# First modulation set in quarters, zero products on TensorE, split row statistics behind the experts, and a new table of priorities

## The chip, the cores and the metric

The kernel runs on one core of one Trainium2 chip. The metric is the device time of one execution in microseconds, the median of some runs. The engines of the core are TensorE (PE in the profile, its weight loads PEld), VectorE (DVE), ScalarE (ACT), GpSimd (POOL) and SyncE (SP), which issues nearly all of the loads.

## The reference

The input is 256 rows of 1024 (`x`), two conditioning vectors and 256 context rows for each of two blocks. Everything is float32. In short:

```python
# block 1
mod = silu(c) @ w_mod + b_mod            # 6 x 1024: sh1 sc1 g1 sh2 sc2 g2
h   = rmsnorm(x, norm1_g) * (1 + sc1) + sh1     # and hc from ctx, with c_ctx
y   = gated_linear_attention(h, hc)      # h @ w_in gives q, k, v, r; gates from w_gate_a, w_gate_b
x   = x + g1 * y
h2  = rmsnorm(x, norm2_g) * (1 + sc2) + sh2
f   = moe(h2)                            # 16 experts, top 2 of the best group of 4
x   = rmsnorm(x + g2 * f, final_g)
# block 2, two layers, each with its own modulation and a context branch
x, xc = ab_layer(x, ctx_2)               # latent attention and grouped attention, gated
x, xc = cd_layer(x, xc)                  # window attention and short convolution, gated
```

## The kernel before, in words

The weights lie in one flat array, cut on the host into pieces of 128 partitions and at most 2048 columns (1 MB), each loaded with one transfer from SyncE's queue. A dense product splits each float32 weight into a rounded part and a rest (`conv`: one ScalarE pass and one VectorE pass over 128x1024), and multiplies three combinations of parts in one-pass format, accumulating in PSUM. `Tjob` gives the product transposed (12 matmuls of 256 columns for each of 8 slices of the contraction), `tokjob` by rows (3 of 512 columns for each 128 rows and slice). The modulation vectors (`gemv`, `gemv_half`) keep float32, with 32 columns of stationary operand, four of them side by side in TensorE's columns.

Nothing runs in the order in which it is written. Every instruction is recorded with a place in the program (`Sched.rec`); stretches are interleaved (`merge`, `Blocks.order`), so that the context branch of block 2 (`cth`) is spread over the experts of block 1, and its last `TAIL` microseconds of TensorE work (`cth2`) are placed behind the experts, into section `t2`. Then `emit` walks through time with a cost for each instruction: an engine takes, among the instructions that could start first, the one with the lowest place plus `later`. `later` comes from the table `PRI`, one number for each section (`op.grp`) and one for each 24 instructions of it. The order found is the order in which each engine's queue, SyncE's included, gets its instructions; on the chip each engine works through its queue in order and waits on semaphores.

The start: `x` is loaded, its rows are normalised (`norm_rows`) and turned by 16 TensorE transposes. The first modulation set (shift and scale of block 1, 8 MB of `w_mod`) is computed in two halves, `gemv_half(0)` and `gemv_half(1)`, each of four 1 MB pieces; half h serves slices 4h to 4h+3 of the contraction. Behind each half one half of the q weights (`gq_h`) is loaded. A slice is modulated on its way out of the transposes' PSUM (`split_evac` under `trans`), multiplied into the gates' first factor (`lps`) and then used by the q, r, k and v products.

The end of the experts: `merge_y` adds each round's output to `facc` (= `x1`), by row tile and half. `overflow` is an instruction of all engines (a branch on a register that is read from memory) that may write `facc`. Then comes section `t2`: `facc` times the final gain (`xn2`), sums of squares of both, a chain of small VectorE instructions for the two reciprocal roots (`rsq`), and the modulated transposes for block 2 (`adaln_T`).

All compute instructions and most loads carry line 384 in the profile, since one helper issues them; the expert loads with an address from a register carry line 2066, and `overflow` line 2222. Rows are told apart by tile names: `w` weight pieces, `cs` the conditioning vectors, `cv` a split weight, `hlh`/`hll` and `hch`/`hcl` the modulated rows in two parts, `xn` is `xn2`.

## Time and profile before

| what | value |
|---|---|
| median of 3 runs | 892.22 us (892.08 to 894.15) |
| the profiled execution | 890.18 us, its span 888.4 us |
| TensorE busy | 844.4 us, 95% of the span |
| VectorE, ScalarE busy | 578.3 us, 416.4 us |
| weight loads of TensorE | 598.1 us (beside matmuls) |
| moved by DMA | 224.14 MB, mean 252 GB/s |
| mean granted TensorE clock | 0.991 |

Busy time of TensorE holds modelled ends of matmuls, so a stretch that is 100% busy may still hold short waits. Of 44 us in which TensorE is idle, most lies in three places: the first 27 us, the experts, and the very end. A wait with "DVEq L2222" or "PEq L2222" is one for the branch of `overflow`.

### The profile page before, as it was taken

Reading aid. Unit: us, or ns where it says so; the run is one execution under the profiler, and the core shown is the slowest. Engines: PE = TensorE matmul, PEld = TensorE weight load, DVE = VectorE, ACT = ScalarE, POOL = GpSimd, SP = SyncE. Lnnn points to the kernel's source line nnn. Section 1 sums busy time; section 2 is a strip of 40 time slices with the busy share of each in tenths; the row PEclk is TensorE's granted clock in tenths of the full one; section 3 lists DMA queues with packets and bytes.
Section 4 is the critical chain, followed back from the end, with each engine's and each line's share of the span. In section 5 each row is a group of like instructions: output and inputs, shape, how many; then the busy total and the mean of one; then the engine's idle time right before and its main releaser. Section 6 shows DMA issues by size and latency. Waiting matters only on the chain. (4 is left out here: it accounts for less than half of the span.)

```text
span 888.4 us, 15257 instructions
## 1 busy us (share of the span) xinstructions
PE 844.4 (95%) x5830; PEld 598.1 (67%) x5830; DVE 578.3 (65%) x1608; ACT 416.4 (47%) x819; POOL 0.9 (0%) x5
## 2 busy tenths in 40 slices
PE   4999999999999999999988995999999999999997
PEld 2677667767875656555633432688876778899986
DVE  2676889428984623444755424989866558899783
ACT  3466545226433222224444433555489715454890
POOL 0000000000000000000000000000000000000000
PEclk9999999999999999999999999899999999999999
DMA  9954961877526999999999998884713203465101
GB/s 381 415 217 181 377 252 58 303 327 285 189 100 229 416 357 374 342 386 371 360 416 373 403 420 317 315 355 143 281 52 142 96 1 142 167 248 204 49 1 48
DMA packets 32834, 224.14 MB, mean 252 GB/s; under 512 B 3568, under 2 KB 3824, under 8 KB 7408
## 3 DMA queue, kind: packets, MB, share of 16 engines
q1 hardware_dynamic: 32608, 222.56, 64.6%
q8 instruction: 48, 0.79, 0.3%
q0 software_dynamic: 144, 0.52, 0.2%
q14 instruction: 34, 0.28, 0.1%
HBM read 222.02 MB, written 1.05 MB: 251 GB/s over the span
## 5 line engine op out<-in xcount | busy, mean ns | idle before, releaser
L384 DVE TENSOR_TENSOR cv<-w,cv 128x1024 fp32r<-128x1024 f32 (+3 forms) x128 | 145.2, 1150 | 26.5 <-ACT cv L384 26.3
L384 ACT ACTIVATE cv<-w 128x1024 fp32r<-128x1024 f32 (+3 forms) x128 | 124.3, 998 | 57.6 <-DMA w<-in_w_dram 36.5
L384 PE MATMUL ps<-hh,cv 128*128 128x256 f32 x576 | 114.4, 288 | 0.2 <-ACT cv L384 0.2
L384 PEld LDWEIGHTS ps<-hh,cv 128*128 128x128 f32 x576 | 92.2, 191 | 5.9 <-issue 4.1
L384 PE MATMUL ps<-w,xg 128*32 128x512 f32 (+1 forms) x544 | 87.8, 605 | 3.3 <-DMA w<-in_w_dram 3.2
L384 PE MATMUL ps<-hl,cv 128*128 128x256 f32 x288 | 81.4, 285 | 0.0
L384 PE MATMUL ps<-cv,hh 128*128 128x512 f32 (+2 forms) x288 | 78.5, 352 | 0.4 <-ACT hh L384 0.4
L384 ACT ACTIVATE t<-ps 128x512 f32<-128x512 f32 (+5 forms) x77 | 36.0, 477 | 84.1 <-PE ps L384 67.4
L384 PE MATMUL ps<-c_col,t 128*128 128x128 f32 x384 | 63.0, 280 | 5.6 <-ACT t L384 4.9
L384 PEld LDWEIGHTS ps<-c_col,t 128*128 128x128 f32 x384 | 44.1, 141 | 33.8 <-ACT t L384 22.0
L384 ACT ACTIVATE t<-ps,s,f 128x512 f32<-128x512 f32 (+1 forms) x80 | 54.9, 690 | 18.6 <-DVE s L384 18.3
L384 PE MATMUL ps<-w,cs 128*32 128x512 f32 (+1 forms) x448 | 50.9, 563 | 12.8 <-DVE s L384 9.1
L384 PE MATMUL ps<-cv,mixh 128*128 128x512 f32 x192 | 60.7, 394 | 0.0
L384 DVE TENSOR_REDUCE s<-ps 128x1 f32<-128x512 f32 (+1 forms) x80 | 45.1, 580 | 20.3 <-PE ps L384 20.1
L384 PE MATMUL ps<-w,t 128*32 128x512 f32 (+1 forms) x320 | 54.2, 599 | 3.6 <-issue 3.0
L384 PEld LDWEIGHTS ps<-hl,cv 128*128 128x128 f32 x288 | 54.9, 191 | 2.8 <-issue 2.4
L384 PEld LDWEIGHTS ps<-cv,hh 128*128 128x128 f32 x288 | 49.7, 189 | 10.0 <-issue 2.4
L384 PEld LDWEIGHTS ps<-w,xg 128*32 128x32 f32 (+1 forms) x544 | 23.0, 118 | 47.1 <-issue 37.0
L384 PE MATMUL ps<-cv,hl 128*128 128x512 f32 (+2 forms) x144 | 49.0, 348 | 0.0
L384 ACT ACTIVATE PT<-ps 128x512 f32<-128x512 f32 (+1 forms) x80 | 39.3, 510 | 20.6 <-PE ps L384 20.3
L384 PE MATMUL ps<-cv,hlh 128*128 128x512 f32 x128 | 42.1, 403 | 0.0
L384 PEld LDWEIGHTS ps<-cv,mixh 128*128 128x128 f32 x192 | 35.7, 188 | 7.3 <-issue 0.4
(269 smaller groups left out, 1515.5 us busy)
## 6 DMA issues: line engine op xcount, KB each, us to landing
w<-in_w_dram SPq DMA_DIRECT2D x198, 1024.0 KB, 7.5
ctx<-in_ctx_dram SPq DMA_DIRECT2D x3, 1024.0 KB, 7.8
w<-in_w_dram SPq DMA_DIRECT2D x4, 576.0 KB, 8.3
x<-in_x_dram SPq DMA_DIRECT2D x2, 1024.0 KB, 7.2
w<-in_w_dram SPq DMA_DIRECT2D x4, 512.0 KB, 3.7
w<-in_w_dram SPq DMA_DIRECT2D x2, 768.0 KB, 9.5
out_dram<-x SPq DMA_DIRECT2D x2, 512.0 KB, 2.6
c_cst<-in_cst_dram SPq DMA_DIRECT2D x1, 528.0 KB, 14.8
```

The source lines that it names most:

```text
L384: op.fn = lambda: getattr(real, fn)(*a, **k)
```

## The change

The first modulation set is cut into four quarters of two 1 MB pieces (`modq{q}_{k4}`: four slices of the contraction with 128 columns for each of the four column groups). Quarter q serves slices 2q and 2q+1. Behind each quarter come, in program order, half-size loads (512 KB) of the q weights and of the first half of the r weights, one step of transposes (`trans_step`), and those slices' share of the two products. The bank pairs of both products (`pl`, `pr`) are held from the start. The scale is formed for both rows of modulation with one instruction a quarter (`A1`).

`busy` multiplies a tile of zeros into a PSUM bank that nothing reads (`idle`): 20 products of 512 columns ahead of the first quarter, and two of 256 columns after each of its eight slices.

Behind the experts the products with the final gain and the sums of squares are taken by halves of 512 columns, with one more addition. `TAIL` goes from 1 to 6. The r block is no longer interleaved with the context's modulation (`GLASEQ`).

The planner walks four times, each time over the order that the last walk found and with a table of its own (`PRIS`, four tables in place of one); nearly every number of the first table differs from `PRI`. It plans loads at 410 bytes a nanosecond instead of 380, and an expert load of 1 MB at 2557 ns instead of 2759 ns. The tables are cut here to their first lines.

```diff
--- before.py
+++ after.py
@@ -102,10 +102,10 @@
                 if b or s:
                     out[f"mod{b}_{s}_{kt}"] = m[:, kt, s * 2048:(s + 1) * 2048]
 
-    m = _kt(mods[0])[:, :, :2048].reshape(128, 8, 2, 2, 512)
-    for h in range(2):
-        for k2 in range(4):
-            out[f"modh{h}_{k2}"] = m[:, 2 * k2:2 * k2 + 2, :, h]
+    m = _kt(mods[0])[:, :, :2048].reshape(128, 8, 2, 4, 256)
+    for q in range(4):
+        for k4 in range(2):
+            out[f"modq{q}_{k4}"] = m[:, 4 * k4:4 * k4 + 4, :, q]
 
     def two(name, w):
         w = _kt(w)
...
-PRI = {
-    '': -1355, ('', 0): -400, ('', 2): 35, ('DB', 0): -400, ('DB', 3): -1630, ('DBc', 0): 1610, ('DG', 0): -210,
-    ('DG', 1): -100, ('DG', 2): 75, ('DG', 3): -265, ('DG', 4): -575, ('DGc', 0): 1575, ('Da', 1): -800,
...
-}
...
-TAIL = 1.0
+PRIS = [
+    {
+      '': -1160, ('DB', 0): -600, ('DB', 3): 370, ('DB', 4): 705, ('DG', 0): -160, ('DG', 1): 700, ('DG', 2): 110,
+      ('DG', 3): -365, ('DG', 4): -2170, ('DGc', 0): -800, ('Da', 1): -800, ('Da', 11): 3300, ('Da', 12): 1160,
...
+    },
+    {
+      '': 490, ('', 0): -590, ('', 1): -980, ('DB', 0): -45, ('DB', 1): -75, ('DB', 2): -2390, ('DB', 3): 1255,
+      ('DB', 4): -715, ('DBc', 0): -1390, ('DG', 0): 1715, ('DG', 1): -735, ('DG', 2): -1455, ('DG', 3): -400,
...
+    },
...
+TAIL = 6.0
...
@@ -277,6 +449,7 @@
 
 DMAW = 0.5
 XM = 0
+WARM = 20
 WPE = 0.0
 WACT = 40.0
 WDVE = 40.0
@@ -295,11 +468,11 @@
 NA = 8
 CTXSEQ = "CKgGqsk ba"
 CDSEQ = "kqc+x gB a+G o"
-GLASEQ = "N q r+M k+l1 K v+L+2 R+3 f"
+GLASEQ = "N q r M k+l1 K v+L+2 R+3 f"
 
 
 class Op:
-    __slots__ = ("eng", "fn", "acc", "cost", "lat", "preds", "npred", "succs", "tiles", "name", "later", "cols", "table", "grp", "tiled")
+    __slots__ = ("eng", "fn", "acc", "cost", "lat", "preds", "npred", "succs", "tiles", "name", "later", "cols", "table", "grp", "tiled", "key")
 
 
 class Sched:
@@ -409,7 +582,7 @@
     def _cost(self, eng, fn, out, a, k):
         n = self._free(out)
         if fn == "dma_start":
-            return out.partition_size() * n * 4 / 380.0
+            return out.partition_size() * n * 4 / 410.0
         if eng == "PE":
             r32 = a[1].dtype == F32R
             if fn == "transpose":
@@ -501,12 +674,21 @@
         out += lst[j:]
         self.cur[i0:i1] = out
 
-    def emit(self, reorder=True, window=3000):
-        ops = self.main
+    def emit(self):
+
         seen = {}
-        for op in ops:
+        for op in self.main:
             k = seen[op.grp] = seen.get(op.grp, -1) + 1
-            op.later += PRI.get(op.grp, 0) + PRI.get((op.grp, k // 24), 0)
+            op.key = op.grp, k // 24
+        for pri in PRIS:
+            for op in self.main:
+                op.later = pri.get(op.grp, 0) + pri.get(op.key, 0)
+            order = self._pass(self.main)
+            self.main = [self.main[i] for i in order]
+        for op in self.main:
+            op.fn()
+
+    def _pass(self, ops, window=3000):
         hist = {}
         for i, op in enumerate(ops):
             op.preds, op.succs = {}, []
@@ -527,10 +709,6 @@
                         h[:] = [x for x in h if x[0] == i or not (
                             r[0] <= x[1][0] and x[1][1] <= r[1] and r[2] <= x[1][2] and x[1][3] <= r[3])]
                 (hw if wr else hr).append((i, r))
-        if not reorder:
-            for op in ops:
-                op.fn()
-            return
         n = len(ops)
         for i, op in enumerate(ops):
             op.npred = len(op.preds)
@@ -698,10 +876,7 @@
                     ready[o2.eng].append(j)
         self.predicted = max(fin)
         self.busy = {e: sum(o.cost for o in ops if o.eng == e) for e in engs}
-        self.order, self.st = order, st
-        self.ret = {}
-        for i in order:
-            self.ret[i] = ops[i].fn()
+        return order
 
 
 class Blocks:
@@ -893,27 +1068,44 @@
             V.tensor_tensor(o[:, :, :, v], src[:, :, :, v], bias, op=OP.add)
         yield
 
-    def gemv_half(h):
+    A1 = fix([8, 2], F32, "f")
+    zero = t2([512], F32R, "z")
+    V.tensor_scalar(zero, cs[0].rearrange("p a b -> p (a b)")[:, 0:1].to_broadcast([128, 512]), 0.0, None, op0=OP.mult)
+    idle = psum()
+
+    def busy(n, w):
+
+        for _ in range(n):
+            mm(idle[:, :w], zero[:, :128], zero[:, :w], True, True)
+
+    sch.sec = "wu"
+    busy(WARM, 512)
+    sch.sec = ""
+
+    def gemv_quarter(q):
 
         ps = psum()
-        for k2 in range(4):
-            w = load(f"modh{h}_{k2}")
-            for kt in (2 * k2, 2 * k2 + 1):
+        for k4 in range(2):
+            w = load(f"modq{q}_{k4}")
+            for k in range(4):
+                kt = 4 * k4 + k
                 with sch.together():
                     for g in range(4):
-                        o = (kt % 2) * 1024 + g * 256
-                        mm(ps[32 * g:32 * g + 32, :256], cs[0][:, kt, :], w[:, o:o + 256], kt == 0, kt == 7)
-        r = t2([256])
-        S.activation(r, ps[:, :256], AF.Copy)
+                        o = k * 512 + g * 128
+                        mm(ps[32 * g:32 * g + 32, :128], cs[0][:, kt, :], w[:, o:o + 128], kt == 0, kt == 7)
+                    if q == 0:
+                        busy(2, 256)
+        r = t2([128])
+        S.activation(r, ps[:, :128], AF.Copy)
         pt = psum()
-        for j in range(2):
-            PE.transpose(pt[:, j * 128:(j + 1) * 128], r[:, j * 128:(j + 1) * 128], ident)
-        o = modc[:, 0, 0].rearrange("p (a h g j) v -> p a h g j v", a=2, h=2, g=2)[:, :, h]
-        bias = col("bm0")[:, :16].rearrange("p (a h g j) -> p a h g j", a=2, h=2, g=2)[:, :, h]
-        src = pt[:, :256].rearrange("p (j a g r) -> p a g j r", j=2, a=2, g=2)
-        for v in range(2):
-            for a in (1, 0):
-                V.tensor_tensor(o[:, a, :, :, v], src[:, a, :, :, v], bias[:, a], op=OP.add)
+        PE.transpose(pt[:, :128], r, ident)
+        o = modc[:, 0, 0].rearrange("p (a q j) v -> p a q j v", a=2, q=4)[:, :, q]
+        bias = col("bm0")[:, :16].rearrange("p (a q j) -> p a q j", a=2, q=4)[:, :, q]
+        V.tensor_tensor(o, pt[:, :128].rearrange("p (a j r) -> p a j r", a=2, j=2)[:, :, :, 0:2],
+                        bias[:, :, :, None].to_broadcast([128, 2, 2, 2]), op=OP.add)
+        c = slice(2 * q, 2 * q + 2)
+        V.scalar_tensor_tensor(A1[:, c, :], modc[:, 0, 0, 8 + 2 * q:10 + 2 * q, :], 1.0,
+                               col("n1")[:, c, None].to_broadcast([128, 2, 2]), op0=OP.add, op1=OP.mult)
 
     def modv(b, vec, v):
         s, h = divmod(vec, 2)
@@ -1003,14 +1195,17 @@
     def trans(tiles, fn):
 
         for k2 in range(4):
-            ps = psum()
-            for j in range(2):
-                for i in range(2):
-                    kt = 2 * k2 + j
-                    PE.transpose(ps[:, j * 256 + i * 128:j * 256 + i * 128 + 128],
-                                 tiles[i][:, kt * 128:(kt + 1) * 128], ident)
-            for j in range(2):
-                fn(2 * k2 + j, ps[:, j * 256:(j + 1) * 256])
+            trans_step(tiles, fn, k2)
+
+    def trans_step(tiles, fn, k2):
+        ps = psum()
+        for j in range(2):
+            for i in range(2):
+                kt = 2 * k2 + j
+                PE.transpose(ps[:, j * 256 + i * 128:j * 256 + i * 128 + 128],
+                             tiles[i][:, kt * 128:(kt + 1) * 128], ident)
+        for j in range(2):
+            fn(2 * k2 + j, ps[:, j * 256:(j + 1) * 256])
 
 
     def conv(src, tag="c"):
@@ -1508,31 +1703,46 @@
 
 
     norm_rows(xl, xl)
-    AB_ = [(fix([8], F32, "f"), modv(0, 0, v)) for v in range(2)]
-    wq = []
-    for h in range(2):
-        gemv_half(h)
-        for v in range(2):
-            c = slice(4 * h, 4 * h + 4)
-            V.scalar_tensor_tensor(AB_[v][0][:, c], modv(0, 1, v)[:, c], 1.0, col("n1")[:, c], op0=OP.add, op1=OP.mult)
-        wq.append(load(f"gq_{h}"))
-    (Al, Bl), (Ac, Bc) = AB_
+    sch.sec = "GM"
     xc = rows2("ctx", SY)
     hl, hc = new_hl("hl"), new_hl("hc")
     wga = col("wga").rearrange("p (k n) -> p k n", k=8)
-    lps = pd()
     bk = Blocks(sch, "G")
-    for (name, h, x_, A, B, o) in (("N", hl, xl, Al, Bl, 0), ("M", hc, xc, Ac, Bc, 256)):
-        bk(name)
-        if h is hc:
-            norm_rows(xc, xc)
-
+    bk("N")
+    lps, pl, pr = pd(), [pd(), pd()], [pd(), pd()]
+
+    def modulated(h, v, o):
         def fn(kt, ps):
             f = t2([256])
-            split_evac(ps, h.hi(kt), h.lo(kt), A[:, kt:kt + 1], B[:, kt:kt + 1], f, ALT and kt % 2)
+            split_evac(ps, h.hi(kt), h.lo(kt), A1[:, kt, v:v + 1], modv(0, 0, v)[:, kt:kt + 1], f, ALT and kt % 2)
             g = kt % 4
             mm(lps[32 * g:32 * g + 32, o:o + 256], wga[:, kt, :], f, kt < 4, kt >= 4)
-        trans(x_, fn)
+        return fn
+
+    early = {"gq": [Tjob(hl, pl)], "gr0": [tokjob(hl, t, pr[t]) for t in range(2)]}
+    blocks = {}
+    for q in range(4):
+        sch.sec = "G0"
+        gemv_quarter(q)
+        c2 = q % 2
+        for n in early:
+            off, ln = W["w"][f"{n}_{q // 2}"]
+            if not c2:
+                blocks[n] = b8([ln], n="w")
+            o_ = c2 * ln // 2
+            SY.dma_start(blocks[n][:, o_:o_ + ln // 2], bass.AP(
+                tensor=D["w"].tensor, offset=D["w"].offset + off + o_, ap=[[ln, 128], [1, ln // 2]]))
+        sch.sec = "GN"
+        trans_step(xl, modulated(hl, 0, 0), q)
+        for n, jobs in early.items():
+            sch.sec = "Gq" if n == "gq" else "Gr"
+            hi, lo = conv(blocks[n].rearrange("p (k n) -> p k n", n=512)[:, 2 * c2:2 * c2 + 2])
+            for k in range(2):
+                for j in jobs:
+                    j(2 * q + k, hi[:, k], lo[:, k], q + k == 0, 2 * q + k == 7)
+    bk("M")
+    norm_rows(xc, xc)
+    trans(xc, modulated(hc, 1, 256))
     low = t2([512], F32R), t2([512], F32R)
     split_evac(lps, *low)
 
@@ -1560,16 +1770,15 @@
     bk("q")
     kq = b8([2, 4, 256], n="kq")
     kT, qT = kq[:, 0], kq[:, 1]
-    pl = [pd(), pd()]
-    dense("gq", 512, [Tjob(hl, pl)], pre=wq)
     for i in range(2):
         S.activation(qT[:, 2 * i:2 * i + 2, :].rearrange("p b t -> p (b t)"), pl[i], AF.Copy, scale=128.0 ** -0.5)
 
     sr = b8([2, 1024], n="sr")
 
     def rproj(rh):
-        pss = [pd(), pd()]
-        dense(f"gr{rh}", 512, [tokjob(hl, 0, pss[0]), tokjob(hl, 1, pss[1])])
+        pss = [pd(), pd()] if rh else pr
+        if rh:
+            dense("gr1", 512, [tokjob(hl, 0, pss[0]), tokjob(hl, 1, pss[1])])
         for t in range(2):
             th = t2([512])
             S.activation(th, pss[t], AF.Tanh, scale=0.5)
@@ -2064,7 +2273,7 @@
             if r not in reg:
                 reg[r] = nc.values_load(eid[0:1, r:r + 1], engines=[mybir.EngineType.SP], min_val=0, max_val=NE - 1)
             nc.sync.dma_start(t, D["w"][bass.ds(reg[r] * step + off, 128 * ln)].rearrange("(p n) -> p n", p=128))
-        sch.special(f, [eid], [t], 2759.0, "SP")
+        sch.special(f, [eid], [t], 2557.0, "SP")
         return t
 
     def loads(ranks, *names):
@@ -2273,11 +2482,15 @@
 
     x2 = b8([2, 1024], n="x2")
     xn2 = b8([2, 1024], n="xn2")
+    s4 = sm([2, 2, 2])
+    for t in range(2):
+        for half in range(2):
+            c = slice(half * 512, half * 512 + 512)
+            V.tensor_tensor(xn2[:, t, c], facc[:, t, c], fg[:, c], op=OP.mult)
+            sumsq(facc[:, t, c], 512, s4[:, half, 0, t:t + 1])
+            (sumsqv if t else sumsq)(xn2[:, t, c], 512, s4[:, half, 1, t:t + 1])
     ss = sm([2, 2])
-    for t in range(2):
-        V.tensor_tensor(xn2[:, t], facc[:, t], fg, op=OP.mult)
-        sumsq(facc[:, t], 1024, ss[:, 0, t:t + 1])
-        (sumsqv if t else sumsq)(xn2[:, t], 1024, ss[:, 1, t:t + 1])
+    V.tensor_tensor(ss, s4[:, 0], s4[:, 1], op=OP.add)
     V.tensor_scalar(ss[:, 0], ss[:, 0], 1.0 / 1024, EPS, op0=OP.mult, op1=OP.add)
     V.tensor_scalar(ss[:, 1], ss[:, 1], 1.0 / 1024, None, op0=OP.mult)
     V.scalar_tensor_tensor(ss[:, 1], ss[:, 0], EPS, ss[:, 1], op0=OP.mult, op1=OP.add)
```

## Rows read from the trace of the kernel before

**Rows 1.** The page, engines' busy time, share of the span, instructions.

```profile
PE 844.4 (95%) x5830; PEld 598.1 (67%) x5830; DVE 578.3 (65%) x1608; ACT 416.4 (47%) x819; POOL 0.9 (0%) x5
```

**Rows 2.** Windows: stretch, length, busy time by engine (instructions), granted clock, DMA share, GB/s.

```profile
0.00:9.00 9.00, 0.00 (x0) 0.00 (x0) 3.60 (x17) 2.66 (x4) 0.20 (x4) 1.00 0.82 319
9.00:26.60 17.60, 14.36 (x130) 7.85 (x130) 6.38 (x21) 6.30 (x9) 0.00 (x0) 1.00 1.01 423
26.60:58.20 31.60, 31.60 (x209) 23.14 (x206) 21.06 (x51) 19.30 (x32) 0.00 (x0) 1.00 0.96 385
58.20:279.00 220.80, 219.01 (x1651) 160.46 (x1649) 160.51 (x394) 99.91 (x168) 0.65 (x1) 1.00 0.59 223
279.00:440.00 161.00, 159.98 (x1025) 92.98 (x1023) 74.31 (x177) 47.13 (x84) 0.00 (x0) 1.00 0.93 360
440.00:547.20 107.20, 91.68 (x620) 39.93 (x612) 49.95 (x186) 49.22 (x137) 0.00 (x0) 0.98 0.98 399
547.20:564.10 16.90, 10.83 (x50) 4.73 (x49) 11.70 (x29) 5.06 (x11) 0.00 (x0) 0.70 0.73 264
564.10:884.70 320.60, 316.90 (x2164) 269.02 (x2164) 250.75 (x739) 186.81 (x375) 0.00 (x0) 1.00 0.40 145
```

**Rows 3.** Waits of SyncE's queue, 279 to 548 us: in total, times, longest.

```profile
SPq L2066 <- PE ps L384: 167.9, 62, 10.7
```

**Rows 4.** Timeline of the first 45 us: start, duration, instructions, idle before.

```profile
9.08 1.93 PE L384 MATMUL ps<-w,cs 128*32 128x256 f32 x16 [9.08 <-DVE s L384]
...
12.30 3.46 PE L384 MATMUL ps<-c_col,x 128*128 128x128 f32 x15 [0.57 <-ACT x L384]
...
15.69 2.80 PE L384 MATMUL ps<-w,cs 128*32 128x256 f32 x48
...
22.72 0.50 PE L384 MATMUL ps<-hlh,cv 128*128 128x256 f32 x2
...
23.67 0.59 PEld L384 LDWEIGHTS ps<-w,cs 128*32 128x32 f32 x16
```

**Rows 5.** Timeline of TensorE, 45 to 62 us.

```profile
45.92 0.28 PE L384 MATMUL ps<-hll,cv 128*128 128x256 f32 x1
46.04 0.40 PE L384 MATMUL ps<-hlh,cv 128*128 128x256 f32 x2
...
46.28 0.63 PE L384 MATMUL ps<-cv,hlh 128*128 128x512 f32 x2
...
49.30 1.14 PE L384 MATMUL ps<-c_col,ctx 128*128 128x128 f32 x9
...
58.20 0.62 PE L384 MATMUL ps<-cv,hch 128*128 128x512 f32 x2
...
59.94 1.09 PE L384 MATMUL ps<-wgh,t 128*128 128x512 f32 x4
```

**Rows 6.** Timeline behind the last expert, 538 to 566 us.

```profile
547.82 2.49 DVE L384 TENSOR_TENSOR x<-x,ps 128x512 f32<-128x512 f32 x4
...
554.59 1.06 ACT L384 ACTIVATE junk<-x 128x1024 bf16<-128x1024 f32 x1 [7.96 <-DVEq L2222]
554.96 2.36 DVE L384 TENSOR_TENSOR xn<-x,fg 128x1024 f32<-128x1024 f32 x2 [4.65 <-DVEq L2222]
...
556.69 1.04 ACT L384 ACTIVATE junk<-xn 128x1024 bf16<-128x1024 f32 x1
...
557.36 1.22 DVE L384 SCALAR_TENSOR_TENSOR junk<-xn 128x1024 bf16<-128x1024 f32 x1
...
558.70 0.17 DVE L384 TENSOR_SCALAR s<-s 128x2 f32<-128x2 f32 x1
...
564.09 0.79 PE L384 MATMUL ps<-cv,hh 128*128 128x288 f32 x4 [0.36 <-ACT hh L384]
```

**Rows 7.** Timeline, 718 to 732 us: sums of squares over 512 columns.

```profile
719.61 0.64 ACT L384 ACTIVATE junk<-x 128x512 bf16<-128x512 f32 x1 [6.29 <-DVE x L384]
...
720.15 0.19 ACT L384 ACTIVATION_READ_ACCUMULATOR junk<-x 128x1 f32 x1
...
720.69 0.68 DVE L384 SCALAR_TENSOR_TENSOR junk<-x 128x512 bf16<-128x512 f32 x1
```

More of the change, by code (lines that the diff above doesn't have):

```diff
@@ L205 @@
 LEAD = 0
-PRI = {
[52 rows of a table removed]
-    'Xbw': 1225, 'Xg': 200, 'Xgc': -970, 'Xk': -105, 'Xkc': -600, 'Xq': 650, 'Xqc': -895, 'Xs': 3675, 'Xsc': 425,
[3 rows of a table removed]
-}
-TAIL = 1.0
+PRIS = [
+    {
[47 rows of a table added]
+      'Dcc': -160, 'Dg': -785, 'Dgc': 10, 'Dkc': -2490, 'Do': 10875, 'Doc': 165, 'Dq': -1220, 'Dqc': 10,
[9 rows of a table added]
+    },
+    {
[38 rows of a table added]
+      ('goc', 0): 300, ('hot', 0): -1405, ('hot', 1): 855, ('moe0', 0): -610, ('moe0', 1): -4775,
[11 rows of a table added]
+      'Lsc': 1590, 'XC': -5, 'XCc': 2130, 'XGc': -1240, 'XK': -50, 'XKc': 800, 'Xa': 245, 'Xb': -210, 'Xbw': 710,
[4 rows of a table added]
+    },
+    {
[56 rows of a table added]
+    },
+    {
[52 rows of a table added]
+    },
+]
+TAIL = 6.0
 APART = 1
```

266 rows, old and new, of tables (PRI, PRIS) are left out of this document.

## The prediction, made before the changed kernel ran

> **What bounds the kernel now.** I read the page's busy times first: TensorE is busy for 844.4 of 888.4 us [rows 1], so only 44 us can come from filling its idle time, unless busy time itself shrinks. The windows by stage come next [rows 2]. TensorE waits 9.0 us for the first weight piece, another 3.2 (17.60 less 14.36) until 26.6 us, and then hardly at all until 440: 1.8 us from 58 to 279, 1.0 from 279 to 440. In the experts' second part (440 to 547) it is idle for 15.5 us while DMA runs at a share of 0.98, and in the 16.9 us behind the last expert for 6.1. From 564 on it is idle for 3.7. So the start is bound by loads, the middle and the last 320 us by TensorE's order, the experts by both: over 279 to 547 the DMA share is 0.93 and then 0.98, 254.8 us of transfers in 268.2 us. The 13.4 us that are missing are SyncE's: it waits 167.9 us in that stretch for TensorE to free a weight buffer [rows 3], and each such wait that outlasts the transfers in flight leaves a hole.
>
> The timeline of the start shows what is done with those 26.6 us [rows 4]. The products with `cs` begin at 9.08. A 1 MB piece takes 1.049 MB at 423 GB/s [rows 2], 2.48 us, so the fourth piece of the first half is there at about 16.5; its products end at 15.69 + 2.80 = 18.49, and the first product of the q block follows at 22.72. That chain of 4.2 us is eviction, transposes, bias, scale, modulation and split.
>
> **The quarters.** A quarter is two pieces, so the first is there at 9.08 + 2.48 = 11.6 instead of 16.5. Its last four slices take about 1.0 us, and with the chain of 4.2 us the first product comes at 16.8, which is 5.9 us earlier. This is the upper bound of the gain; most of it isn't kept, since TensorE has little to do before 16.8. I count work done by 26.6 us. Before: of the 130 instructions [rows 2] 16 are transposes of `x`, worth 0.109 us each at the pace of those of `ctx` (1.14 us for nine, the last one about 0.27 [rows 5]), 1.7 us in all; some 96 are products with `cs` at 2.80/48 = 0.058 us [rows 4], 5.6 us; the rest, at 0.12 us (0.40 less 0.28 [rows 5]), about 2. That is 9.3 us, so 17.3 us were lost. After: 9.1 us before the first piece; about 1.5 between the two pieces (2.48 less four slices); 4.2 of the chain less four transposes of 0.11, so 3.8; and the extra cost of narrower products. Narrow products double the weight loads to 256. Sixteen loads took 0.59 us with the last one's own 0.11 [rows 4], so 0.032 each and 8.2 us, against 128 x 0.058 = 7.4 us now: 0.8 us more. The losses come to 15.2 us, 2.1 less than before. After that TensorE has 5.6 us of products a quarter (24 at 0.12 and 12 at 0.23, by 59.94 against 46.28 [rows 5]) and the gemv's 2 us, against 3 MB of loads in 7.4 us: it stays the later of the two, and the quarters' chains are covered by the products of the quarter before. If a chain is late, TensorE stands for up to its 4.2 us; four chains instead of two make that likelier. I take a gain of 2.0 us, with bounds of 5.9 gained and 2.0 lost.
>
> The Trainium skill, in "TensorE: Matmul & The Clock Gate", section "LDWEIGHTS (loading the stationary operand)", gives a load as its columns divided by 1.2 in nanoseconds. An estimate from that page for 32 columns is 27 ns, or 6.8 us for 256 loads, so by the page the narrow form would cost nothing and the sum below would be -11.2 instead of -10.4 us; by the row it costs the 0.8 us above, and the row decides.
>
> **Loads.** The half-size loads move no byte more, but 512 KB of r weights and the other halves now stand in SyncE's queue ahead of `ctx`, which comes one piece, 2.5 us, later. Its transposes start at about 48 and the first product with it at 58.20 [rows 5]; both now come behind the same products. I take nothing for it, and 2.5 us if they turn out to wait.
>
> **The zeros.** The transposes of `x` run 3.46/15 = 0.231 us apart, those of `ctx` 0.109 [rows 4, 5]. That is the lower of the two clock levels (1.2 GHz) although the granted clock reads 1.00 in that window [rows 2], which lists no earlier fall; before them TensorE had done almost nothing. Twenty zero products of 512 columns take 20 x 0.23 = 4.6 us at the full clock, about 9.7 at half. Begun at some 2 us they end between 7 and 12, beside a first piece at 9.08 and a second at 11.6; at worst 1 us of gemv is late. The two after each slice are 16 x 0.12 = 1.9 us, half of it in the wait for the second piece. What they can give back is 16 x 0.122 = 2.0 us of the transposes, of which only four stand before the first product. I take nothing net, from 1.0 lost to 2.0 gained; both lie within the bounds above.
>
> **The norm by halves.** The first multiplication with the gain starts at 554.96, released by the branch of `overflow`, while the last addition into `facc` ended at 547.82 + 2.49 = 550.31 [rows 6]. So no half can start earlier: the branch may write all of `facc`, and everything queues behind it. What is left is more fixed cost. ScalarE had three passes of 1024 from 554.59 to about 557.9; six passes of 512 at 0.73 us (0.64 to 720.34 with the read-out [rows 7]) take 4.4, to 559.0. VectorE has four multiplications of about 0.62 (2.49/4 [rows 6]) and two sums of about 0.75 [rows 7], 4.0 us, to 559.0, and one more addition of 0.17. The chain that began at 558.70 [rows 6] begins at about 559.3: 0.6 us lost, with bounds of 0.2 and 1.2.
>
> **TAIL.** Five more microseconds of the context branch stand behind the branch, where TensorE is idle for 6.1 of 16.9 us and runs at a granted 0.70 [rows 2]. There they are free if they fit; at the lower clock they may take 10, and their VectorE share may delay the chain to 564.09 by a few us. Taken out of the experts they are worth something only where TensorE is the bound, 161 of the 268 us, so 3 us at most. I take 1.5 gained, with bounds of 4 gained and 3 lost.
>
> **The new order.** Nothing in the trace shows the new tables' order. What it can win is the slack that rows show outside the start and the gap: 13.4 us of DMA among the experts, 1.8 of TensorE's before them, 3.7 behind [rows 2], 18.9 in all. What speaks for a gain is that the planner took 2.76 us for a piece which lands every 2.48, and now takes 2.56: its holes and the chip's will fall nearer together. It can lose as well. I take two fifths, 7.5 us, with bounds of 14 gained and 9 lost (below).
>
> **The sum.** -2.0 + 0.6 - 1.5 - 7.5 = -10.4 us. The profiled execution took 890.18 us, 1.8 more than its span; it would take 879.8, its span 878.0. The median of the runs lies 2.0 above the profiled one, so I forecast 892.2 - 10.4 = 881.8 us. A measurement of this kernel tells changes of about 0.3%, 2.7 us, from none.
>
> **Rivals.** (1) Slower: SyncE's holes grow. The new order lets expert buffers be held longer, and the share over 279 to 547 falls from 0.95 to 0.92, as far below as the better stage stands above. The 254.8 us of transfers then take 277, 8.8 more; without the gain by order the sum stands at 889.3, so 898. It is slower than before beyond noise when the share falls below about 0.93 (254.8/273.8). For it: 167.9 us of such waits [rows 3], so small shifts matter. Against it: transfers fill 0.98 of the second part already, and faster planned loads ask for earlier issues. (2) No change: the early start is eaten by four chains, and the order gives nothing: 0 + 0.6 - 1.5, 891.3. For it: only 9.3 us of work before 26.6 and a chain that is as long for a quarter as for a half. (3) Much faster: the first product's 5.9 us are kept, TAIL gives 4, and the order closes three quarters of its 18.9, 14 us: 892.2 - 23.3 = 868.9. For it: TensorE is idle 15.5 us beside late weights; against it, each of these idle times has another cause.
>
> **Chances.** The forecast (875 to 889) 0.55, rival 3 0.22, rival 2 0.11, rival 1 0.12. Faster by over 0.3%: 0.55 + 0.22 and a little of rival 2, 0.78; within 0.3% 0.11; slower 0.11. The range from 868 to 892 leaves out part of rival 3 (0.07) and rival 1 (0.12); it is wide because the order's term is.
>
> **What would show it.** The first q product at about 17 us instead of 22.72, transposes of `x` 0.11 us apart, and the first product with `hch` 1 to 4 us earlier than 58.20. The chain of small VectorE instructions behind the branch begins about 4.4 us after the first row sum instead of 4.1. The stretch from the first expert load to the branch is shorter than now and has a higher DMA share, while the stage from there to the end keeps its 320 us within 3. The prediction is wrong if the experts' stretch doesn't shrink, if the first quarter's product comes after 20 us, or if the context work behind the branch pushes the first `hh` product back.

## The result: slower by 0.7%, and the profile after

The changed kernel takes 899.11 us (median of 10 runs, 895.99 to 902.92) against 892.15 for the one before: 1.0074 times, 95% interval 1.0051 to 1.0097. I had forecast 881.8. The profiled execution took 899.54 us, 9.4 more than that of before.

The page first, the counterpart of [rows 1]: TensorE is busy 10.1 us longer, with the same share; the 36 products of zeros alone have 11.6 us of busy time.

```profile
PE 854.5 (95%) x5994; PEld 606.4 (68%) x5994; DVE 580.0 (65%) x1610; ACT 415.9 (46%) x827; POOL 0.8 (0%) x5
```

Windows by stage (columns as in [rows 2]; the edges are the changed kernel's own milestones, so stages rather than lines answer to those rows):

```profile
0.00:14.80 14.80, 8.57 (x35) 6.39 (x36) 4.76 (x24) 5.83 (x7) 0.20 (x4) 1.00 0.89 331
14.80:26.60 11.80, 11.72 (x166) 7.78 (x166) 6.07 (x14) 4.00 (x9) 0.00 (x0) 1.00 1.02 418
...
240.00:279.00 39.00, 38.41 (x214) 28.53 (x212) 29.62 (x123) 14.03 (x35) 0.00 (x0) 0.87 0.29 110
279.00:440.00 161.00, 156.76 (x987) 86.31 (x988) 67.38 (x164) 40.24 (x71) 0.00 (x0) 0.99 0.91 360
440.00:557.00 117.00, 97.61 (x650) 46.52 (x649) 55.95 (x192) 49.22 (x129) 0.00 (x0) 0.99 0.98 393
557.00:571.00 14.00, 9.05 (x55) 4.88 (x55) 10.88 (x32) 9.37 (x28) 0.00 (x0) 0.76 0.49 181
571.00:894.00 323.00, 320.45 (x2189) 269.75 (x2185) 252.01 (x748) 187.45 (x382) 0.00 (x0) 1.00 0.40 148
```

TensorE's idle time of the first 26.6 us is halved (6.3 us where it was 12.2), but products of zeros fill it: without their 11.6 us TensorE is busy for 8.7 us by then, where it was for 14.4. The experts end at 557 instead of 547, and the last stage keeps its length. So the loss stands ahead of it. Timeline of TensorE at the start, to be held against [rows 4] and, its last line, [rows 5]:

```profile
5.10 5.22 PE L557 MATMUL ps<-z 128*128 128x512 f32 x12 [5.10 <-DVE z L557]
11.45 0.55 PE L557 MATMUL ps<-c_col,x 128*128 128x128 f32 x3 [1.13 <-ACT x L557]
...
14.78 0.43 PE L557 MATMUL ps<-w,cs 128*32 128x128 f32 x8
15.14 0.51 PE L557 MATMUL ps<-z 128*128 128x256 f32 x2
...
22.36 1.08 PE L557 MATMUL ps<-w,cs 128*32 128x128 f32 x32
...
23.94 0.39 PE L557 MATMUL ps<-hlh,cv 128*128 128x256 f32 x1
...
54.63 0.63 PE L557 MATMUL ps<-cv,hch 128*128 128x512 f32 x2
```

The first q product comes at 23.94, later than before (22.72), since the transposes of `x` stand ahead of the first slice on TensorE and wait for ScalarE's norm, and each slice is followed by 0.4 us of zeros. The first product with `hch` is 3.6 us earlier, as forecast, but less work stands ahead of it: 18 of the 32 products of the gates' first factor (`t,c_col`) instead of all 32, and 12 of the 16 transposes of `ctx`. With the old order behind the same start (e16, below) it comes at 58.15. Up to the end of the 32 routing products (`s,t`) nothing is left: 244.9 us before, 248.0 after. Profiled executions scatter here: 248.0 to 250.2 us in the six with the new order up to this point (two of them without some or all of the zeros), 244.9 to 245.7 in four with the old one. TensorE by lines, 239 us to that point, before and then after:

```profile
L384 PE MATMUL ps<-s,t 128*128 128x16 f32 x32 | 3.9, 258 | 0.1
L384 PE MATMUL ps<-cv,hh 128*128 128x512 f32 x5 | 2.0, 426 | 0.0
L384 PE MATMUL ps<-cv,hl 128*128 128x512 f32 x2 | 0.8, 392 | 0.0
```

```profile
L557 PE MATMUL ps<-s,t 128*128 128x16 f32 x32 | 3.9, 262 | 0.1
L557 PE MATMUL ps<-cv,hh 128*128 128x512 f32 x9 | 3.1, 403 | 0.0
L557 PE MATMUL ps<-cv,hl 128*128 128x512 f32 x4 | 1.6, 411 | 0.0
```

Six more products of a later branch (`cv,hh` and `cv,hl`) stand ahead of the routing, in the chain that leads to the experts: 1.9 us by these lines, which count overlapping ends, and an estimate of 1.4 by the 0.23 us by which the starts of such products lie apart.

SyncE's wait for the experts' ids (from 240 us on; before, then after) is 8.6 us longer; the first expert load goes out at 271.2 us instead of 261.2, and the last product with `xg` comes 9.8 us later:

```profile
SPq L2065 <- DVE t L384: 20.7, 1, 20.7
```

```profile
SPq L2274 <- DVE oh L557: 29.3, 1, 29.3
```

This was my first explanation, theory A: the ids are late, the experts are bound by transfers, so all of the delay reaches the end. It fell. Windows within the experts, before and then after, show a second place:

```profile
279.00:320.00 41.00, 40.84 (x290) 23.91 (x288) 20.72 (x61) 11.63 (x26) 0.00 (x0) 1.00 0.90 350
320.00:360.00 40.00, 40.00 (x280) 22.09 (x279) 15.35 (x24) 10.57 (x16) 0.00 (x0) 1.00 0.93 365
```

```profile
279.00:320.00 41.00, 40.50 (x276) 22.22 (x280) 17.15 (x55) 7.88 (x20) 0.00 (x0) 1.00 0.92 366
320.00:360.00 40.00, 37.70 (x269) 21.47 (x262) 17.19 (x29) 11.10 (x17) 0.00 (x0) 0.96 0.75 292
```

The DMA share falls to 0.75 there. I counted the weights from the first expert load on by their landings (the end of a transfer): the first is 10.1 us late, the 7th only 3.0 (in the old order it had waited for TensorE to free a buffer), the 25th again 12.6, behind a hole of 8.9 us, the 97th 9.8.

### The profile page after: what moved, and what is told of

The parts are those of the page before. It is cut to its first block, busy times and chain, and to the rows that moved or that the text cites. A ratio compares the mean times of both kernels' runs of the same rounds, so it can differ in the third digit from the quotient of the medians.

```text
span 897.7 us, 15610 instructions
## 1 busy us (share of the span) xinstructions
PE 854.5 (95%) x5994; PEld 606.4 (68%) x5994; DVE 580.0 (65%) x1610; ACT 415.9 (46%) x827; POOL 0.8 (0%) x5
## 5 line engine op out<-in xcount | busy, mean ns | idle before, releaser
L557 PE MATMUL ps<-hh,cv 128*128 128x256 f32 x576 | 111.7, 288 | 2.5 <-ACT cv L557 2.5
L557 PE MATMUL ps<-w,xg 128*32 128x512 f32 (+1 forms) x544 | 89.9, 616 | 3.6 <-DMA w<-in_w_dram 3.5
L557 ACT ACTIVATE t<-ps 128x512 f32<-128x512 f32 (+6 forms) x79 | 36.5, 470 | 78.0 <-PE ps L557 60.7
L557 PE MATMUL ps<-c_col,t 128*128 128x128 f32 x384 | 65.1, 280 | 5.1 <-ACT t L557 5.1
L557 PE MATMUL ps<-w,t 128*32 128x512 f32 (+1 forms) x320 | 56.7, 613 | 7.4 <-DMA w<-in_w_dram 4.5
L557 PEld LDWEIGHTS ps<-cv,hh 128*128 128x128 f32 x288 | 49.2, 192 | 11.2 <-issue 3.2
L557 PEld LDWEIGHTS ps<-w,xg 128*32 128x32 f32 (+1 forms) x544 | 22.2, 118 | 44.3 <-issue 33.7
L557 DVE TENSOR_TENSOR t<-ps,bc 128x512 f32<-128x512 f32 x28 | 19.0, 686 | 45.7 <-PE ps L557 45.7
L557 PE MATMUL ps<-cv,hlh 128*128 128x512 f32 x128 | 43.9, 413 | 0.1
```

The lines of the kernel that those rows point to most:

```text
L557: op.fn = lambda: getattr(real, fn)(*a, **k)
```

## The experiments

Ratios are to the kernel before, with 95% intervals.

**Single edits.** The code in this section is cut to what matters. e1 ranks the ids' operations earlier in the last walk and lets it plan again; e8 moves only these operations on VectorE, in the finished order; e7 moves only one block on TensorE; e2 makes the ids late in the kernel before.

```
e1  for op in self.ids: op.later -= 6000        # last walk
e8  key[i] -= 300 places for the ids' operations # finished order
e7  48 products into ps755, ps756: behind the down products into ps465, ps466
e2  -V.tensor_copy(eid, ef)
    +V.scalar_tensor_tensor(eid, exs..., 0.0, ef, op0=mult, op1=add)   # behind the overflow sum exs
```

> The changed kernel, with one difference in the last walk of its planner: the operations of the section that turns the routing weights into the ids of the chosen experts are ranked 6000 places earlier, so that VectorE works them ahead of the overflow counts and the other work that now stands among them. The rest of the walk is planned again around that, so places elsewhere move too. Theory A (the ids come late, so the weights' transfers start late, and a stage bound by transfers carries the delay to the end): the wait of SyncE ahead of the first expert load, 29.3 us in the changed kernel, falls by 4 to 8 us, the first load is issued at 263 to 267 us in place of 271.4, and the time falls by about the same, to 891 to 895 us. Rival B (the order of the work among the experts, or the clock behind the small routing products, costs the time): the first load may come earlier, but the last product of the last expert does not, and the time stays at 897 to 901 us.

> The changed kernel with one edit of the order on VectorE: the operations from the routing sums to the integer ids stand in one row ahead of the overflow counts, with nothing else moved. Theory A (the late ids carry all of the 10 us through): the first expert load is issued 6 to 9 us earlier than 271.4 us and the time falls by 5 to 8 us, to 891 to 894 us. Theory A2 (the ids' delay counts only for the part that the first weights do not wait for TensorE anyway; in the two traces the seventh weight lands only 3.2 us later in the changed kernel where the first lands 10.3 us later): the time falls by 1 to 3.5 us.

> The changed kernel with one edit of the order on TensorE: the block of 48 products of 256 columns that stands at 325.7 to 331.7 us, in the middle of the first round of four experts, is put behind the down products of that round. All else keeps its order. Theory A2: SyncE's wait of 10.7 us there shrinks by 4 to 8 us, the hole of 8.9 us between two landings (343.9 to 352.8) goes, all later landings come 3 to 6 us earlier and the time falls by as much, to 893 to 896 us. Rival E (the stage regains by itself what a hole loses, since the weights wait for TensorE anyway): the hole goes, and the last landing and the time stay within 1.5 us.

> The kernel before, old order table and old features, with one edit: the copy that makes the experts' ids an integer tile is replaced by an operation that also reads the overflow sum (times zero), so that the ids wait for the overflow counts. The values are the same. Theory A: the first expert load is issued 3 to 9 us later than 261.2 us, the last weights land as much later than 547.2 us, and the time rises by as much, to 895 to 901 us. Rival B (the experts' stage has slack that takes up a late start): the first load is late by as much, but the time rises by less than 1.5 us.

e1: 907.61 us, 1.0162 (1.0125 to 1.0199). e8: 906.37, 1.0134 (1.0107 to 1.0160). The first load goes out 6.7 and 7.0 us earlier than in the changed kernel, and both are slower than it, against theory A and A2 alike. In e8 the one-hot rows that feed the gather now stand behind the ids on VectorE, the first product with `xg` comes at 287.2 us instead of 280.1 (its routing also ended 3.3 us late, and TensorE ran at the lower clock from 263 to 277 us in that execution, so not all of the 7.1 us is the order), and the weights wait for it. e7: 903.87, 1.0131 (1.0094 to 1.0168). TensorE, e7:

```profile
332.82 3.68 PE L557 MATMUL ps<-w,xg 128*64 128x512 f32 x8 [4.10 <-DMA w<-in_w_dram]
336.44 2.43 PE L557 MATMUL ps<-w,t 128*32 128x512 f32 x16
```

With the block gone TensorE comes early to a product of the next round, waits 4.1 us for its weights, and the down products that would free buffers queue behind it. The share over 320 to 360 us stays 0.75, with a granted clock of 0.91. TensorE's order waits for loads, and the loads' order for TensorE; A2's gain doesn't come, and rival E's "no change" was still too good. e2: 898.39, 1.0053 (1.0031 to 1.0074): the time lies in theory A's range, but in the old order 8.8 us of delay of the first load cost only about half (4.7 us by the ratio; the 97th weight lands 4.4 us late).

**Zeros.** e3 leaves out all 36 products of zeros, e4 the 16 behind slices.

```
 mm(idle[:, :w], zero[:, :128], zero[:, :w], True, True)
+sch.cur[-1].fn = lambda: None     # e4: only if w == 256
```

> The changed kernel with the same order of everything else, but without all 36 products of zeros (nothing reads them). Theory C (the zeros hold up the first quarter and cost what the quarters bring): the first q product comes 2 to 5 us earlier than 23.9 us even though the transposes of x run at the half clock again, and the time falls by 1.5 to 4 us. Theory A: what the start gains is taken up ahead of the routing, since the ids' chain sits on VectorE behind work that the order put there; the first expert load moves by less than 1.5 us and the time stays within 2 us of 899.

> The changed kernel with the same order, without the 16 products of zeros that stand behind the slices of the first quarter; the 20 warm-up products stay. Theory C: a slice of the first quarter takes 0.2 us in place of 0.79, the first q product comes 3 to 5 us earlier than 23.9 us with the clock full, and the time falls by 2 to 5 us, more than without any zeros. Theory A: as for the run without any zeros, the gain at the start does not reach the first expert load, and the time stays within 2 us of 899.

899.13 us, 1.0085 (1.0058 to 1.0112), and 897.82, 1.0050 (1.0019 to 1.0081), both around the change's own 1.0074. The first q product does come earlier, at 21.0 and 22.1 us, as theory C has it, but the time doesn't follow. Theory C falls: the zeros aren't the loss.

**Features and order apart, planned.** e5 has the changed kernel's operations with the old table, prices and tail; e6 the old operations with the four new tables.

```
e5  PRIS = [PRI]; TAIL = 1.0; 380 and 2759 for 410 and 2557
e6  PRIS, four walks, TAIL = 6.0, 410 and 2557 in the kernel before
```

> The changed kernel's quarters, zeros and split norm, but planned in one walk with the old order table and the old prices (old tail as well). Theory A2 (the new order is what costs: late ids and a hole in the transfers at 344 to 353 us): the first expert load and the landing of the weights stay within 4 us of the kernel before, and the time is 888 to 895 us. Rival C (the zeros and the quarters cost it): the time stays at 897 to 901 us.

> The kernel before with its halves and its unsplit norm and without zeros, but planned with the four new tables in four walks, the new prices and the new tail. Theory A2: the order alone costs what the change costs or more, since it was not found for these operations: 897 to 905 us. Rival C: without the zeros and the quarters, the time is 888 to 894 us.

902.12 us, 1.0106 (1.0074 to 1.0138), and 952.49, 1.0656 (1.0630 to 1.0682). Both lie outside every range above. Neither tells features from order, since the planner makes a third and a fourth order from them: a table fits one list of operations.

**Grafts.** So I took the planner out. The finished orders of both kernels are lists of nearly the same operations. A graft keeps its kernel's own order up to a cut and sorts all that is left by the other kernel's order, as far as data and buffers allow; a new operation of the split norm stands ahead of the one that follows it on its engine.

```
 order = self._pass(self.main)
+if pri is PRIS[-1]: order = self._sorted(self.main, order, RANK)
 # RANK: own place up to the cut, then the other kernel's place
```

> A graft: the changed kernel (quarters, zeros, split norm) in its own order up to the last operation of the routing products (1,647 of 6,488 operations; the kernel before has done the same ones but for six at its own such point), and from there every operation in the order of the kernel before. Theory R (the order from the routing on costs the time): only what the start brings is left; the routing products end 3.3 us later than in the kernel before, so 892 to 896 us, 3 to 7 us under the changed kernel. Rival T (the order up to the routing costs it, and what follows only carries it): 897 to 901 us, as the changed kernel.

> The mirror of that graft: the kernel before (halves, no zeros, unsplit norm) in its own order up to the last operation of the routing products, and from there every operation in the order of the changed kernel. Theory R: the new order of the rest costs its 4 to 7 us here too, 895 to 900 us. Rival T: 890 to 894 us.

> The graft cut earlier: the changed kernel in its own order up to the last transpose step of the first modulation (334 operations, some 40 us), and from there everything in the order of the kernel before. Theory Q (the quarters bring their 3 us, which the new order between 55 and 240 us gives back): the first product of the second half of the modulation stays 2 to 4 us earlier than 58.2 us, the routing ends 1 to 3 us earlier than in the kernel before, and the time is 887 to 891 us. Rival: what the quarters bring is lost again before the routing in the old order too, or at the experts' weights, which then wait for buffers: 891 to 894 us.

> The same early graft without the 16 products of zeros behind the slices of the first quarter (nothing reads them). Theory C (the zeros hold up the first quarter): 2 to 4 us less than the graft with them, 884 to 888 us. Rival: within 1.5 us of the graft with them.

> The graft cut at 334 operations (quarters, split norm, old order behind) without any of the 36 products of zeros. If the zeros only stand in TensorE's way: the first products start at the landing of the first piece, and the time is 1.5 to 3.5 us under that graft's 892.2. If the full clock that they buy pays for them: the clock rises later than 9.4 us, and the time stays within 1.5 us of it.

| graft | us | ratio |
|---|---|---|
| e9: new order to the routing, old behind | 897.15 | 1.0050 (1.0032 to 1.0069) |
| e10: old order to the routing, new behind | 895.43 | 1.0031 (1.0014 to 1.0048) |
| e11: new to 40 us, with all features; old behind | 892.21 | 1.0000 (0.9984 to 1.0016) |
| e12: e11 without the slices' zeros | 893.78 | 1.0021 (1.0000 to 1.0042) |
| e16: e11 without any zeros | 893.13 | 1.0000 (0.9977 to 1.0023) |

This splits features from order. Quarters, zeros and split norm together are worth nothing that the intervals show (e11 within 1.4 us, e16 within 2.1). The new order costs 0.50% ahead of the routing (e9) and 0.31% behind it (e10), each give or take 0.2%; the sum, 7.2 us of 892, is the change's 6.6 within its interval, if the two parts simply add. Theory R and rival T were both half right. Windows of e16 and then of the kernel before show that the start brings nothing by 58 us and that both run alike from there:

```profile
0.00:58.00 58.00, 44.27 (x461) 33.44 (x462) 32.64 (x88) 29.37 (x47) 0.20 (x4) 1.00 0.97 389
58.00:244.90 186.90, 185.13 (x1463) 138.25 (x1462) 136.29 (x290) 88.48 (x141) 0.65 (x1) 1.00 0.61 235
```

```profile
0.00:58.00 58.00, 45.76 (x333) 30.83 (x334) 30.84 (x89) 28.10 (x45) 0.20 (x4) 1.00 0.96 387
58.00:244.90 186.90, 185.11 (x1462) 138.05 (x1461) 136.34 (x291) 88.71 (x141) 0.65 (x1) 1.00 0.62 236
```

In e16 the first q product comes at 20.80 and the first r product at 23.5 (before 22.72 and 36.7), yet TensorE is idle for 13.7 of the first 58 us instead of 12.2. e11 has 51.45 us of busy time up to 58 us, 7.2 more than e16: the zeros fill idle time, and little more.

**Cuts elsewhere.** Three more grafts: e13 cut inside the first mixer, e14 and e15 behind the ids instead of ahead of them.

> The graft of the changed kernel's start onto the old order, cut at the last operation of the first mixer's low-rank gate (814 operations of 6,488, between the cut at 334, which measured 1.000 of the kernel before, and the cut at 1,647, which measured 1.005). If the new order of the first products and of the gate (the first product on the log gates came 13.5 us later in the changed kernel) costs the 5 us: 895 to 899 us. If the order behind it, the mixer's chunks and the products on its way out, costs them: 891 to 894 us.

> The same graft cut behind the section that makes the experts' ids (1,834 operations), so that the ids are made in the new order. Theory A (late ids cost time): the first expert load is issued some 4 us later than in the graft cut ahead of that section and the time is 2 to 5 us above that graft's 897.2. Rival (the first weights wait for TensorE anyway): within 1.5 us of it.

> The mirror: the kernel before in its own order up to and with the ids, then the new order. Theory A: the first expert load comes back to about 261 to 263 us and the 3 us that the graft with new ids lost are regained, 890 to 893 us. Rival (the hole in the transfers between the 18th and the 24th weight costs them): the hole of 6 us stays and the time is 894 to 897 us.

e13: 905.12 us, 1.0141 (1.0098 to 1.0184), outside both forecasts and worse than either order, so two halves of a mixer's orders don't fit, and where the 0.50% lies ahead of the routing stays open; the six products above are read from rows and weren't tested alone. e14: 899.88, 1.0072 (1.0048 to 1.0097), which can't be told from e9. e15: 897.32, 1.0039 (1.0016 to 1.0063), no faster than e10, although its first load goes out at 261.9 us and not 268.5. Windows of e15 within the experts:

```profile
279.00:320.00 41.00, 38.72 (x269) 20.86 (x268) 16.16 (x52) 8.88 (x21) 0.00 (x0) 1.00 0.88 333
320.00:360.00 40.00, 39.69 (x281) 22.67 (x282) 17.31 (x29) 9.91 (x16) 0.00 (x0) 1.00 0.82 324
```

The 7th weight lands 0.1 us behind the kernel before, the 19th 1.6, the 25th 7.8: with punctual ids the hole is still there. Theory A is refuted for the new order. In e9, with the old order there, the lag stays between 4.2 and 8.3 us up to the 97th weight, and the share over 320 to 360 us is 0.95. So the hole belongs to the new order of the first round of four experts. But that it makes the 0.31% behind the routing isn't shown: e7, which was to close it, opened another, and e3's profiled execution (893.83 us, the fastest of its 12) has the same hole, of 9.2 us, and makes it good. Its 25th weight lands 5.3 us late, its 97th only 1.5. Windows of e3:

```profile
320.00:360.00 40.00, 38.78 (x275) 22.36 (x273) 15.77 (x29) 10.22 (x17) 0.00 (x0) 1.00 0.81 328
240.00:543.00 303.00, 282.90 (x1829) 156.21 (x1827) 150.15 (x470) 102.28 (x232) 0.00 (x0) 1.00 0.87 349
```

Unlike the changed kernel's, this execution keeps the full clock up to 543 us (see the last section).

**The context.** In e16 ScalarE and VectorE wait for the context ahead of the second quarter's eviction, whose products end at 22.2 us (timeline):

```profile
23.50 1.06 ACT L562 ACTIVATE junk<-ctx 128x1024 bf16<-128x1024 f32 x1 [3.41 <-DMA ctx<-in_ctx_dram]
23.50 1.23 DVE L562 SCALAR_TENSOR_TENSOR junk<-ctx 128x1024 bf16<-128x1024 f32 x1 [2.60 <-DMA ctx<-in_ctx_dram]
...
24.56 0.26 ACT L562 ACTIVATE t<-ps 128x128 f32<-128x128 f32 x1
```

The Trainium skill ("TensorE: Matmul & The Clock Gate", section "Architectural detail: the array is 16× 32×32, not 1× 128×128") says that these two engines work strictly in order; the lines agree. e17 and e18 move the context, with 12 zeros back in e18.

```
 DMA order: ctx, c_cst, rows behind the third quarter's two pieces
 the context's norm behind the third quarter's eviction (ScalarE, VectorE)
```

> The graft with quarters, no zeros and the old order behind, with the loads of the context, a constant table and a row table put behind the third quarter's pieces in SyncE's queue, and the operations that normalise the context behind the third quarter's eviction on ScalarE and VectorE. Theory F (the wait on the context ahead of the second quarter's eviction takes the gain): the second quarter's eviction comes some 4 us earlier than 24.6 us, TensorE's idle time up to 58 us falls from 13.7 us by 2 to 4 us, and the time by as much, to 889 to 891 us. Rival G (the transfers up to 58 us set the end of the stage): the idle time moves behind 30 us, the first product of the context's half stays at 58 to 59 us, and the time stays at 892 to 894 us.

> The same with the first 12 of the warm-up products of zeros put back, which end ahead of the first transposes of x; the 24 others stay out. If the full clock at the start is worth something by itself: the transposes of x cost 0.28 us in place of 0.39 and the time is 1 to 2 us under the run without zeros. Rival: within 1 us of it, since what TensorE then does is set by the pieces' landing.

899.61 us, 1.0067 (1.0045 to 1.0090), and 898.11, 1.0067 (1.0047 to 1.0086). Windows of e17:

```profile
0.00:27.00 27.00, 15.10 (x184) 11.67 (x184) 11.53 (x38) 10.85 (x16) 0.20 (x4) 1.00 0.93 371
27.00:58.00 31.00, 26.47 (x251) 20.19 (x252) 16.78 (x42) 14.04 (x22) 0.00 (x0) 0.94 1.00 399
```

The second quarter's eviction comes at 22.22 us and TensorE gains 1.8 us by 27 (e16: 13.33 busy), but then waits for the context's half (2.7 us), loses 4.5 by 58 (e16: 30.94), and does it at a granted 0.94. The first `hch` product is 5.7 us later than in e16, the routing's end 5.7, the median about 6. Theory F falls. Rival G has the bound right and its times wrong: the first `hch` product comes at 63.8 us and not at 58 to 59, and the time isn't 892 to 894. DMA runs at a share of 0.93 to 1.00 all the time to 58 us, and a piece put forward put another back. In this kernel 5.7 us lost at 58 us are still there at the end. e18's ratio is e17's, as its rival has it; but in its profiled execution the clock falls at 12.3 us, among the transposes of `x`, so what a full clock there is worth stays open. No version beat the kernel before.

## Why the prediction was wrong

**The new order**, the largest term, failed: forecast 7.5 us gained, bounds 14 gained to 9 lost. The grafts measure about 4.5 lost ahead of the routing and 2.8 behind. I reckoned a share of idle time that any order might fill; the trace of before had no row on this order, and a term of both signs should have had its middle near zero. That the order costs the time is shown; how it does so is not. Two things are in rows, work of a later branch ahead of the routing (1.4 to 1.9 us) and the hole at 320 to 360 us, but neither was removed and the time regained.

**Rival 1** forecast 898, and its number came by luck more than by its reason. Its condition wasn't met: the share over 279 to 547 us fell only from 0.95 to 0.94 by the windows, not to 0.92, and SyncE's waits for TensorE's buffers grew by only 4.9 us. The counterpart of [rows 3], 279 to 548 us:

```profile
SPq L2275 <- PE ps L557: 172.8, 66, 10.7
```

It named one real hole, at 320 to 360 us, but the larger part of the loss arrives from ahead of the experts, which it left out.

**The quarters**, 2.0 us forecast, give 0.0 (e16). Its interval of some 2 us either way can't rule the forecast out, but the rows can: TensorE's idle time up to 58 us grows by 1.5 us, and the routing ends at 244.6 us instead of 244.9. Wrong was the queue: I had the first slice at 9.1 us, but in the new order the transposes of `x` stand ahead of it and wait for ScalarE until 11.2 (first slice 14.4 in e16, 14.8 in the changed kernel). The price of the narrow products was wrong too. They start in fours, and by their starts in the trace the fours lie 0.109 us apart at the full clock, 0.027 each and 7.0 us for 256, where I had 0.032 and 8.2. The wide ones of before lie 0.216 apart, 0.054 each and 6.9 for 128, where I had 0.058 and 7.4: I had counted the last product's own time into the pace. So the narrow form costs 0.1 us and not 0.8. The 0.027 agrees with the 27 ns that I estimated from the Trainium skill, "TensorE: Matmul & The Clock Gate", section "LDWEIGHTS (loading the stationary operand)".

**Loads** at nothing held in the changed kernel. Its first quarter is so late that ScalarE comes to the context without a wait (timeline):

```profile
23.48 0.40 ACT L557 ACTIVATE hlh<-t 128x256 fp32r<-128x256 f32 x1
23.83 1.06 ACT L557 ACTIVATE junk<-ctx 128x1024 bf16<-128x1024 f32 x1
...
25.38 0.28 ACT L557 ACTIVATE t<-ps 128x128 f32<-128x128 f32 x1 [0.40 <-PE ps L557]
```

Only without the zeros does the context hold the second quarter's eviction up, from 22.2 to 24.56 us (e16).

**The zeros**, nothing net: right. The transposes ran 0.11 us apart, as forecast (1.17 us for nine, less the last one's own 0.27, over eight), and neither e12 nor e16 is faster than e11.

**The norm by halves**, 0.6 lost, wasn't measured alone. Timeline behind the branch, after, against [rows 6]:

```profile
561.47 2.49 DVE L557 TENSOR_TENSOR xn<-x,fg 128x512 f32<-128x512 f32 x4 [2.60 <-DVEq L2431]
...
565.30 0.16 DVE L557 TENSOR_TENSOR s<-s 128x4 f32<-128x4 f32 x1
...
572.81 0.77 PE L557 MATMUL ps<-cv,hh 128*128 128x288 f32 x4
```

The small chain starts 3.83 us behind the first multiplication (before 3.74). Counted from the first ScalarE pass (561.26) it is 4.0 us, not my 4.4.

**TAIL**, 1.5 gained, wasn't measured alone either; by these rows it is worth nothing. The first `hh` product is pushed back, as the prediction feared: 11.3 us behind the first multiplication into `xn` instead of 9.1. In return that multiplication comes 2.1 us sooner behind the last addition (a wait of 2.60 instead of 4.65). The two cancel: from that addition's end to the `hh` product it is 13.9 us, before 13.8. What the work taken out of the experts gave there isn't shown.

## What to carry to other kernels

Where a change brings both features and a new order, graft one finished order onto the other and compare; planning again with the old table costs as much as what is to be measured (e5 against e11). An early start was worth here what TensorE's idle time up to the next point that transfers set shrank by (e16, e17), not the earlier first product. In a stage where the loads' queue waits for TensorE and TensorE for loads, moving one wait mostly makes the next: follow the n-th landing, not the first.

## What was not expected of the hardware

In the changed kernel the granted clock over 240 to 279 us is 0.87, against 1.00 before: TensorE falls to the lower level (1.2 GHz) from 248.8 to 252.2 and from 262.5 to 269.3 us, behind the 32 routing products of 16 columns, which stand in one row from 244.1 to 248.0 us with TensorE busy all the time. The same row doesn't always bring it: in the profiled executions of e3 and e14 the clock stays full there. It isn't the whole loss: the profiled executions of e10 (896.44 us) and e14 (895.42) keep the full clock up to 542 and 451 us and are slower than 892 all the same. But part of the loss goes with it. I sorted 34 runs of the changed order (the changed kernel, e3 and e4) and 112 of the kernel before by their mean granted clock: at 0.992 or more the medians are 896.6 and 891.1 us, 5.5 apart, and below that 900.8 and 892.6, 8.2 apart. The order costs most of the loss at the higher clock too; how much of the rest is a lower clock at a bad place stays open. And the changed order's runs spread wider: 12 runs of e3 lie between 893.8 and 905.8 us, 29 of the kernel before between 889.8 and 898.7.
